# Moving the transposes, the query load and one combination in the attention rows of a hybrid transformer layer

## Chip, cores and metric

The kernel runs on one core of a Trainium2 chip. The metric is device time in microseconds (us) of one execution. Median of three runs before: 2978.12 us (2976.74 to 2979.64).

Engine names are those of the profile: PE is TensorE (matrix products; PEld its weight loads), DVE is VectorE, ACT is ScalarE, POOL is GpSimd, SP is SyncE, which issues most DMA transfers. Each engine executes its own instructions in the order in which the program gives them. PE writes to PSUM, which has eight banks of 512 floats on each of 128 partitions.

## What is computed

One transformer layer, for 256 prompt tokens and 2048 latent tokens. A joint projection gives q, k, v and Fourier channels; the first three go through differential attention, the Fourier channels through a two-dimensional DFT; then come an output projection, a residual, and a squared-ReLU feed-forward net. Latent tokens attend to 512 cached and 2048 latent keys. The part of the reference that the change touches is this:

```python
def one_block(qblk):
    s = jnp.einsum('bqhmd,bkhmd->bhmqk', qblk, k).astype(jnp.float32) * scale
    p = jax.nn.softmax(s, axis=-1)
    a = p[:, :, 0] - lam * p[:, :, 1]
    return jnp.einsum('bhqk,bkhe->bqhe', a.astype(v.dtype), v)
```

There are 4 heads, two score maps m for each head (head dimension 64), and values of width 128. All data are float32; products are made from a high and a low part of one operand or of both (fp32r), so that a float32 product takes several passes.

## The kernel before, in words

The program runs through projection and DFT, attention (from about 568 to 1325 us of the profile), output projection and feed-forward net. The change lies in attention alone.

**Rows and steps.** Attention for the latent tokens has 32 rows: 4 heads by 8 groups of 256 queries (class Group; tile names such as Ss, P0s, pts carry no row number in the profile). A row has two halves j of 128 queries and two maps m, so four softmax sets of 128 x 2560 scores. A set is made in five blocks of 512 keys:

- `fill` (L920): two matmuls on PE into one PSUM bank S. The tag S has five banks, one for each block of a set, so block n of a set can be written when block n of the set before has been read by its exponential.
- `rowmax` (L925): DVE reduces each block to its maximum. `comb` (L928) combines five maxima and negates.
- `exp` (L944): ACT writes exp(S - max) into P0 (m = 0) or P1 (m = 1) and sums it.

After both maps of a half, `combine` forms P0 + factor x P1: small operations on DVE (L948, L949), the factor (L950) and a square (L951), and then the large part. On POOL that is a tensor_scalar (L966) and an addition (L967), first on columns 0 to 1023, then on 1024 to 2559. For the first `vcomb` blocks of 512 columns of the second half of a row, DVE does it instead with one operation a block (L956). `vcomb` is 5 in the very first row and in the very last, 0 elsewhere.

Then the combined weights are transposed and multiplied by the values. `tr` (L976) transposes four 128 x 128 squares on PE into one bank pts (the tag has two banks): one call is a group of two key tiles. `ah` (L982) copies that bank on ACT, `al` (L987) subtracts the copy on DVE to get the low part, and `mul` (L86 to L88, or L1001 and L1008 for two groups that go in one float32 product) multiplies into the bank po.

At a row's end, `o1` (L1012) copies po on ACT, `o2` (L1016) transposes it on PE, `o3` (L1020) copies it on DVE, `o4` (L1026) squares and sums it on ACT (two operations with their sums), `o5` (L1029, L83) and `o6` (L1035) normalise it, and SP stores it to att (L1036). `qload` (L897) has SP load the 256 queries of a row into one of three buffers Q. The prompt's own small attention (class Prompt, one row a head) is woven in between.

**Order.** The order is written out by hand: every call is added to a list with a planned time, and the list, sorted by that time, is the order in which each engine gets its instructions (`manual_schedule`). T is the planned length of a step and u = T / 5. Only the sequence follows from these times; nothing waits for a clock. A row takes four steps. While a row's four sets are made, the sets of the next row are already under way and those of an earlier row are transposed and multiplied; the loop `for q in range(4)` lays a row's ten transpose groups over four steps:

- Step A (q = 0): key tiles 0 and 2; step B (q = 1): 4, 6, 8; step C (q = 2): 10 and 12; step D (q = 3): 14, 16, 18. The number is `kb`, the first of two key tiles.
- In A and C PE makes the five blocks of a later row's set with m = 1 (KS1s) while ACT makes exponentials with m = 0 (P0s); in B and D it is the other way round (KS0s, P1s).
- Products of a step's groups come at the end of the step after it. `o4` of an earlier row comes in step C, behind the second copy `ah`.

PE's order in a step before the change is then: block 1, block 2, first transposes, blocks 3 and 4, second transposes, block 5, (B and D: third transposes), products. In B `o2` follows the first transposes. The planned times that set it, in units of u from the step's start, are blocks at 0.76, 1.42, 2.08, 2.74 and 3.40, and the transposes at:

```python
tr_t, ah_t, al_t = [1.5, 2.8], [3.3, 3.8], [4.6, 5.2]              # A and C
tr_t, ah_t, al_t = [1.5, 2.8, 3.86], [3.3, 3.8, 4.4], [None, 4.6, 5.2]   # B and D
```

Of the kernel before, what the change touches and what calls it, by code (L numbers as in the profile page):

```python
# [40 lines left out]
def body(tc, a, out):  # L41
    nc = tc.nc
    ctx = ExitStack()
    with ctx:
# [796 lines left out]
        with ExitStack() as c3_:  # L841
# [12 lines left out]
            class Head:  # L854
                def __init__(self, s, h):
                    self.s, self.h, self.nm = s, h, f"{'sp'[s]}{h}"
                    self.nk = NK[s]
                    self.nkt, self.nbk = self.nk // P, (self.nk + 511) // 512
                    self.ng = (NS, NP)[s] // 256
                    self.tok0 = (NP, 0)[s] // P  # L860
                    self.hc = slice(h * P, h * P + P)
# [21 lines left out]
            class Group:  # L883
                def __init__(self, hd, g):
                    self.hd, self.g, self.nm = hd, g, f"{hd.nm}_{g}"
                    self.S, self.mx, self.sm, self.p0, self.p1, self.tot = {}, {}, {}, {}, {}, {}
                    self.pt, self.A = {}, {}
                    self.po, self.half = None, []
                    self.nmul = 0
                    self.edge = 20 * g - 1 if hd.h == hd.s == 0 and g < 2 else None  # L890
                    self.last = hd.h == H - 1 and g == NS // 256 - 1

                    self.vcomb = 5 if self.last else 5 if hd.h == hd.s == g == 0 else 0

                def qload(self):
                    self.Q = at.tile([P, 2, 2, 256], F32R, tag="Q", name=f"Q{self.nm}", bufs=3)
# [196 lines left out]
            def add(t, fn, *args):  # L1093
                ev.append((t, len(ev), fn, args))

            T = TSTEP
            u = T / 5.0
# [11 lines left out]
            for h in range(H):  # L1109
                hd, hp = Head(0, h), Head(1, h)  # L1110
                base = h * 32 * T
                add(base - 18 * T + 0.7 if h else -3.04 * T, hd.load_k)
                add(base - 14 * T + 0.7 if h else 0.9 * T, hd.load_v)
                add(base - 13 * T + 0.7 if h else 0.91 * T, hp.load_k)
                add(base - 13 * T + 0.71 if h else 0.92 * T, hp.load_v)
                gp, r = Prompt(hp, 0), base + 10 * T
                add(r - 2 * T, gp.qload)
                for j in range(2):
                    for t, fn in ((5.25, gp.scores), (5.85, gp.rowmax), (6.33, gp.exp), (8.0, gp.combine)):
                        add(r + t * u, fn, j)  # L1120
                    r += 2 * T
                for t, fn, *args in ((5.25, gp.tr, 0), (6.33, gp.ah), (6.95, gp.al), (15.25, gp.mul), (16.33, gp.o1),
                                     (25.25, gp.o2), (25.9, gp.o3), (27.32, gp.o4), (28.557, gp.o5), (29.0, gp.o6)):
                    add(r + t * u, fn, *args)
                for g in range(hd.ng):
                    gr = Group(hd, g)
                    add(base - 2 * T + 0.6 * u if base else -3.03 * T, gr.qload)
                    for st in range(4):
                        j, m = divmod(st, 2)
                        t0 = base + st * T  # L1130
                        for b in range(hd.nbk):
                            add(t0 - T + (0.76 + 0.66 * b) * u, gr.fill, j, m, b)
                            add(t0 - T + (1.26 + 0.66 * b) * u, gr.rowmax, j, m, b)
                            add(t0 + 0.66 * b * u, gr.exp, j, m, b)
                        add(t0 - 0.45 * u, gr.comb, j, m)
                        if m:
                            add(t0 + 5.9 * u, gr.combine, j)
                    kbs = list(range(0, hd.nkt, 2))
                    for q in range(4):
                        w = base + (AVS + q) * T  # L1140
                        if q % 2 == 0:
                            order = [kbs.pop(0) for _ in range(2)]
                            tr_t, ah_t, al_t = [1.5, 2.8], [3.3, 3.8], [4.6, 5.2]
                        else:
                            order = [kbs.pop(0) for _ in range(3)]
                            tr_t, ah_t, al_t = [1.5, 2.8, 3.86], [3.3, 3.8, 4.4], [None, 4.6, 5.2]
                        for n, kb in enumerate(order):
                            add(w + tr_t[n] * u, gr.tr, kb)
                            add(w + ah_t[n] * u, gr.ah, kb)
                            if al_t[n]:  # L1150
                                add(w + al_t[n] * u, gr.al, kb)
                            add(w + T + (3.9 + 0.01 * n) * u, gr.mul, kb)
                            if q == 3 and not n:
                                add(w + 3.95 * u, gr.mul_part, kb)
                    w = base + (AVS + 5) * T + 1.0 * u
                    for t, fn in ((0, gr.o1), (0.75, gr.o2), (0.95 if gr.last else 4.25, gr.o3), (8.5, gr.o4), (9.2, gr.o5), (9.6, gr.o6)):
                        if gr.last and t > 5:
                            LASTO.append(fn)
                        else:
                            add(w + t * u, fn)  # L1160
                    base += 4 * T
# [340 lines left out]
        with c5r, ExitStack() as c5:  # L1502
# [155 lines left out]
            with tc.manual_schedule():  # L1658
                for n, (q, p) in enumerate(ITEMS):
# [10 lines left out]
                    fn, args = FINISH.get(n, (None, ()))  # L1670
# [61 lines left out]
        with ExitStack() as c6:  # L1732
# [62 lines left out]
            with tc.manual_schedule():  # L1795
                pend, NM, loaded, KS = None, 7 * 24, 4, []
                for i in range(7):
                    for b in range(3):
                        ps = [pp.tile([P, 512], F32, tag="ps", name=f"ps{i}_{b}_{j}", bufs=6) for j in range(3)]
                        for k in range(16):  # L1800
# [19 lines left out]
                            if (i, b) == (6, 2) and 9 <= k < 12:  # L1820

                                j = k - 9
                                u = U3[6 + j]
# [14 lines left out]
                for j in range(3):  # L1838
                    t = 6 + j
# [76 lines left out]
```

## Time and profile before

| what | us |
|---|---|
| median of three runs | 2978.12 |
| profiled execution, its own time | 2977.31 |
| its span from first to last instruction | 2975.5 |
| PE busy | 2914.6 |
| DVE busy | 2025.9 |
| ACT busy | 1580.1 |
| POOL busy | 1022.5 |
| attention 800 to 900 us: PE, DVE, ACT, POOL busy of 100 | 97.75, 88.94, 89.51, 89.89 |
| attention 567 to 600 us: PE, DVE, ACT, POOL busy of 33 | 23.77, 27.56, 22.07, 9.71 |

Busy times are shares of the span on which an engine executes something. Matmuls overlap in PE's pipeline and their ends are modelled, so PE's busy time is no measure of how much of its peak it reaches. The chain of work that ended last is followed back from the last instruction, at each point to what released it or to the instruction before it on the same engine; what is not on it has slack. In a timeline, several equal instructions stand in one line (x4 = four of them) with the start of the first and the time until the end of the last, and square brackets give the idle time ahead of them and who ended it. A block of scores is two matmuls, so x2 is one block, x4 two.

### The profile page before, as it was taken

What the parts mean: (1) busy time and instruction counts of PE and PEld (TensorE: products, weight loads), DVE (VectorE), ACT (ScalarE), POOL (GpSimd) and SP (SyncE); (2) the same over time, 40 slices, a digit from 0 to 9 for tenths busy, and PEclk for the clock granted to TensorE, in tenths of its full rate; (3) what the DMA queues carried; (4) which work ended last, traced back from release to release, by engine and by line L of the source; (5) the groups of instructions that cost most, each with busy time, mean ns of one, the idle gap of its engine ahead of it and who ended that gap; (6) DMA issues with size and microseconds to landing.
All of it is one profiled execution on the core that took longest, in us unless ns stands there. A gap on an engine that the chain in (4) does not pass through costs nothing.

```text
span 2975.5 us, 43868 instructions
## 1 busy us (share of the span) xinstructions
PE 2914.6 (98%) x15481; PEld 2512.7 (84%) x15481; DVE 2025.9 (68%) x3379; ACT 1580.1 (53%) x3540; POOL 1022.5 (34%) x839
## 2 busy tenths in 40 slices
PE   8999999999999999999999999999999999999999
PEld 5888887778888888878888999999999888888887
DVE  6666775789888888865458778777776344344554
ACT  4333322688888889964346556556555322232221
POOL 1111112178888988851222333333332000000000
PEclk9999999999999999999999999999999999999999
DMA  7777878512120121215686677676666454445563
GB/s 274 204 195 205 226 195 250 193 52 76 42 110 28 70 84 35 86 58 157 202 251 215 218 239 226 219 238 214 221 200 228 145 171 162 138 145 174 195 215 106
DMA packets 394413, 495.58 MB, mean 167 GB/s; under 512 B 26403, under 2 KB 307056, under 8 KB 391122
## 3 DMA queue, kind: packets, MB, share of 16 engines
q1 hardware_dynamic: 386560, 477.63, 50.4%
q0 software_dynamic: 2992, 7.28, 0.8%
q10 hardware_dynamic: 4642, 7.88, 0.8%
q8 instruction: 122, 2.00, 0.3%
q14 instruction: 97, 0.79, 0.1%
HBM read 315.20 MB, written 179.57 MB: 166 GB/s over the span
## 4 chain that ended last, share of the span: by engine, by line
PE 90%; DVE 3%; ACT 2%; DMA 2%; issue 1%; POOL 1%; SPq 0%; ACTq 0%; DVEq 0%; POOLq 0%
PE Ss L920 10%; PE ps L86 8%; PE ps L87 8%; PE ps L88 8%; PE pj L86 4%; PE pj L88 4%; PE pj L87 4%; PE pts L976 4%; PE po L88 4%; PE po L86 4%; PE po L87 4%; PE pA L1542 2%; PE pA L1543 2%; PE pB L1542 2%; PE pA L1544 2%; PE pC L1544 2%
## 5 line engine op out<-in xcount | busy, mean ns | idle before, releaser
L925 DVE TENSOR_REDUCE mxs<-Ss 128x1 f32<-128x512 f32 x640 | 421.8, 687 | 80.4 <-PE Ss L920 69.9
L1237 DVE TENSOR_TENSOR sl<-sr,sh 128x768 fp32r<-128x768 f32 x168 | 161.7, 963 | 339.9 <-ACT sh L1236 339.4
L967 POOL TENSOR_TENSOR P0s<-P0s,P1s 128x1024 f32<-128x1024 f32 x124 | 365.3, 2946 | 10.3
L1236 ACT CAST sh<-sr 128x768 fp32r<-128x768 f32 x168 | 140.2, 835 | 424.9 <-PE ps L87 424.9
L1584 POOL TENSOR_TENSOR gs<-g,g 128x384 f32<-128x384 f32 x48 | 70.2, 1464 | 483.3 <-ACT g L1554 392.3
L944 ACT ACTIVATE P1s<-Ss,mxs 128x512 f32<-128x512 f32 x320 | 217.3, 694 | 35.6 <-DVE mxs L928 33.4
L86 PE MATMUL pj<-wh,hh 128*128 128x512 f32 x576 | 229.6, 399 | 0.7 <-ACT fo L374 0.7
L87 PE MATMUL ps<-tlT,sh 128*128 128x512 f32 x585 | 229.3, 392 | 0.0
L86 PE MATMUL ps<-thT,sh 128*128 128x512 f32 x585 | 229.2, 392 | 0.0
L87 PE MATMUL pj<-wl,hh 128*128 128x512 f32 x576 | 227.5, 395 | 0.5 <-DVE wl L496 0.5
L88 PE MATMUL ps<-thT,sl 128*128 128x512 f32 x585 | 227.7, 389 | 0.0
L88 PE MATMUL pj<-wh,hl 128*128 128x512 f32 x576 | 226.4, 394 | 0.0
L944 ACT ACTIVATE P0s<-Ss,mxs 128x512 f32<-128x512 f32 x320 | 215.8, 696 | 6.5 <-DVE mxs L928 6.3
L920 PE MATMUL Ss<-KS0s,Qs 128*128 128x512 f32 x640 | 201.8, 424 | 16.9 <-ACT P1s L944 15.6
L920 PE MATMUL Ss<-KS1s,Qs 128*128 128x512 f32 x640 | 210.9, 434 | 4.8 <-ACT P0s L944 4.0
L976 PEld LDWEIGHTS pts<-ident,P0s 128*128 128x128 f32 x1280 | 159.1, 141 | 45.4 <-ACT ahs L982 2.8
L976 PE MATMUL pts<-ident,P0s 128*128 128x128 f32 x1280 | 191.7, 273 | 3.4 <-DVE als L987 1.8
L1553 ACT ACTIVATE g<-uz 128x384 f32<-128x384 f32 x144 | 75.8, 527 | 207.3 <-DVE uz L1576 180.7
L982 ACT CAST ahs<-pts 128x512 fp32r<-128x512 f32 x256 | 151.3, 593 | 47.9 <-PE pts L976 39.7
L987 DVE TENSOR_TENSOR als<-pts,ahs 128x512 fp32r<-128x512 f32 x256 | 165.8, 681 | 11.5 <-ACT ahs L982 11.5
L966 POOL TENSOR_SCALAR P1s<-P1s,tots 128x1024 f32<-128x1024 f32 x124 | 166.8, 1346 | 5.6
L86 PE MATMUL ps<-ophT,sh 128*128 128x512 f32 x423 | 165.9, 392 | 1.1 <-DVE uz L1576 1.1
(615 smaller groups left out, 8248.2 us busy)
## 6 DMA issues: line engine op xcount, KB each, us to landing
sr<-sd SPq DMA_DIRECT2D x84, 768.0 KB, 4.4
a<-in_w SPq DMA_DIRECT2D x184, 256.0 KB, 4.0
sd<-gs SPq DMA_DIRECT2D x192, 192.0 KB, 1.9
sd<-g SPq DMA_DIRECT2D x144, 192.0 KB, 4.0
wm<-in_w_mod SPq DMA_DIRECT2D x32, 512.0 KB, 4.9
Qs<-qd SPq DMA_DIRECT2D x32, 512.0 KB, 3.5
b<-in_w SPq DMA_DIRECT2D x64, 256.0 KB, 4.9
b<-tsum SPq DMA_DIRECT2D x64, 256.0 KB, 4.6
```

The source lines that it names most:

```text
L86: nc.tensor.matmul(ps, lh, rh, start=first, stop=False)
L87: nc.tensor.matmul(ps, lh, rl, start=False, stop=False)
L88: nc.tensor.matmul(ps, ll, rh, start=False, stop=last)
L920: nc.tensor.matmul(S[:, :w], self.Q[:, x, m, j * P:j * P + P], self.hd.KS[m][:, b * 512:b * 512 + w], start=(x == 0), stop=(x == 1))
L925: nc.vector.tensor_reduce(self.mx[j][:, m, b:b + 1], self.S[j, m, b], axis=AX.X, op=ALU.max)
L944: nc.scalar.activation(dst, S, AF.Exp, bias=self.mx[j][:, m, 6:7], accum_out=self.sm[j][:, m, b:b + 1])
L966: nc.gpsimd.tensor_scalar(p, p, tot[:, 3:4], 0.0, op0=ALU.mult, op1=ALU.add)
L967: nc.gpsimd.tensor_add(d, d, p)
L976: nc.tensor.transpose(pt[:, c:c + P], self.p0[j][:, (kb + t) * P:(kb + t + 1) * P], ident)
L982: nc.scalar.copy(t, self.pt[kb])
L987: nc.vector.tensor_sub(t, self.pt[kb], f32(self.A[kb][0]))
L1237: nc.vector.tensor_sub(lo, src, f32(hi))
```

## The change

- The first transposes of every step are planned at 2.1 u instead of 1.5 u, which is behind the third score block instead of the second. In A and C the second transposes are planned at 3.45 u instead of 2.8 u, behind the fifth block instead of the fourth.
- `o2` is planned 0.4 u later (1.15 instead of 0.75), so it stays behind the first transposes of step B; in the last row `o3` moves along (1.35 instead of 0.95).
- `qload` is planned one step earlier (base - 3 T instead of base - 2 T) in all rows but the first.
- In the very first row `vcomb` is 2 instead of 5: DVE combines columns 0 to 1023 of the second half with two operations, POOL columns 1024 to 2559 with L966 and L967.

In the built program PE's order differs by these exchanges in 31 steps A and 30 steps each of B, C and D, DVE has three operations fewer (L956) and POOL two more, ACT's order is the same, and on SP's queue a query load now stands ahead of the two stores of att that came before it.

```diff
-                    self.vcomb = 5 if self.last else 5 if hd.h == hd.s == g == 0 else 0
+                    self.vcomb = 5 if self.last else 2 if hd.h == hd.s == g == 0 else 0
...
-                    add(base - 2 * T + 0.6 * u if base else -3.03 * T, gr.qload)
+                    add(base - 3 * T + 0.6 * u if base else -3.03 * T, gr.qload)
...
-                            tr_t, ah_t, al_t = [1.5, 2.8], [3.3, 3.8], [4.6, 5.2]
+                            tr_t, ah_t, al_t = [2.1, 3.45], [3.3, 3.8], [4.6, 5.2]
...
-                            tr_t, ah_t, al_t = [1.5, 2.8, 3.86], [3.3, 3.8, 4.4], [None, 4.6, 5.2]
+                            tr_t, ah_t, al_t = [2.1, 2.8, 3.86], [3.3, 3.8, 4.4], [None, 4.6, 5.2]
...
-                    for t, fn in ((0, gr.o1), (0.75, gr.o2), (0.95 if gr.last else 4.25, gr.o3), (8.5, gr.o4), (9.2, gr.o5), (9.6, gr.o6)):
+                    for t, fn in ((0, gr.o1), (1.15, gr.o2), (1.35 if gr.last else 4.25, gr.o3), (8.5, gr.o4), (9.2, gr.o5), (9.6, gr.o6)):
```

## The prediction

> **What bounds the kernel now.** I read the page first: engine totals, then the chain of work that ended last. TensorE (PE) is busy 98% of the span and is 90% of that chain, so only what shortens or lengthens PE's own order of work counts.
>
> ```profile
> PE   2914.6 (98%) x15481; PEld 2512.7 (84%) x15481; DVE 2025.9 (68%) x3379; ACT 1580.1 (53%) x3540; POOL 1022.5 (34%) x839
> ...
> PE 90%; DVE 3%; ACT 2%; DMA 2%; issue 1%; POOL 1%; SPq 0%; ACTq 0%; DVEq 0%; POOLq 0%
> ```
>
> All edits lie in attention, so I next took the same chain in order of time over a few rows (a row is 256 queries of one head). Columns: start, length, what. A row has four steps; A and C transpose two groups (pts), B and D three. Shown are the first two score blocks of A, B, C, D and of the next A (775.79 is C), with all of C up to its fifth block.
>
> ```profile
> 764.78 1.12 PE Ss L920 x4
> ...
> 770.20 1.21 PE Ss L920 x4
> ...
> 775.79 1.40 PE Ss L920 x4
> 777.19 0.44 PE pts L976 x4
> 777.62 0.93 PE Ss L920 x4
> 778.55 0.44 PE pts L976 x4
> 778.99 0.46 PE Ss L920 x2
> ...
> 781.73 0.97 PE Ss L920 x4
> ...
> 787.00 1.18 PE Ss L920 x4
> ```
>
> Two score blocks (x4, two matmuls each) cost 0.93 when nothing holds them, 0.465 a block; a transpose group costs 0.435. The opening pairs of A, B, C, D take 1.12, 1.21, 1.40 and 0.97, so they hold waits of 0.19, 0.28, 0.47 and 0.04: 0.98 us a row. A row takes 787.00 - 764.78 = 22.22, so 21.24 is PE work and 0.98 is all that better order could win: at most 30 us over 30 to 31 rows.
>
> What the pair waits for is seen in the timeline of a step C and the start of its D (start, length, engine, line; brackets give idle time and who ended it).
>
> ```profile
> 800.40 2.05 DVE L925 TENSOR_REDUCE mxs<-Ss 128x1 f32<-128x512 f32 x3 [0.21 <-PE Ss L920]
> ...
> 800.67 0.60 PE L976 MATMUL pts<-ident,P0s 128*128 128x128 f32 x4
> ...
> 801.02 0.71 PE L920 MATMUL Ss<-KS1s,Qs 128*128 128x512 f32 x2
> ...
> 801.36 0.59 ACT L982 CAST ahs<-pts 128x512 fp32r<-128x512 f32 x1 [0.20 <-PE pts L976]
> ...
> 802.27 0.31 ACT L1026 ACTIVATE osqs<-os 128x128 f32<-128x128 f32 x1
> ...
> 802.49 0.19 ACT L1026 ACTIVATION_READ_ACCUMULATOR osqs<-os 128x1 f32 x1
> 802.49 0.16 DVE L928 TENSOR_REDUCE mxs<-mxs 128x1 f32<-128x5 f32 x1
> ...
> 802.74 0.69 ACT L944 ACTIVATE P1s<-Ss,mxs 128x512 f32<-128x512 f32 x1
> ...
> 803.42 0.68 ACT L944 ACTIVATE P1s<-Ss,mxs 128x512 f32<-128x512 f32 x1
> ...
> 804.24 0.30 PEld L920 LDWEIGHTS Ss<-KS0s,Qs 128*128 128x128 f32 x2 [0.21 <-ACT P1s L944]
> ```
>
> There are five score banks, so block n of a step needs block n of the step before to have been exponentiated: the second exp ends at 804.10, the second block's weights start at 804.24. Exps follow each other every 0.67 to 0.68 (802.74, 803.42). The first exp waits for the combined maximum (802.49), that for the last of five reduces, and that for the fifth block: three reduces from 800.40 in 2.05 put the last start near 801.76, 0.74 after the fifth block's 801.02. So the loop is: fifth block, reduce, maximum, exps, next step's second block. Its other side is PE's work from the fifth block to that second block.
>
> **First transposes behind the third block.** Instruction counts on PE stay; the built order swaps places in 31 steps A and 30 each of B, C and D (while the last rows are transposed there are no scores left), and ScalarE's order is unchanged. Before, the first transposes (0.435) stood between the second and third block, so the third came 0.465 + 0.435 = 0.90 after the second, later than the exps' 0.67. Now it can come 0.465 after, and its bank is free 0.67 after: where the second block waited, the third waits another 0.205, and the transposes that could fill it stand behind it. The fourth follows at 0.90, past its exp. The earlier third reduce wins nothing if the last reduce hangs on the fifth block. Cost: +0.205 in A, +0.205 in C. The second output transposes (o2) move along in B, at no change of work.
>
> **Second transposes behind the fifth block (A and C).** The fifth block comes earlier relative to PE's remaining work by 0.435. The reduces now limit by a little: five with their data there take 3.09, 0.60 apart, while the blocks are 0.465 apart, so 0.135 is lost.
>
> ```profile
> 804.88 3.09 DVE L925 TENSOR_REDUCE mxs<-Ss 128x1 f32<-128x512 f32 x5
> ```
>
> So the second block of the following step (B, D) waits 0.30 less. In B: 0.28 goes to nothing with 0.02 to spare, and its third block then waits 0.205 - 0.02 = 0.185; gain 0.095. In D 0.04 would go, but ScalarE interferes. The second copy (ahs) cannot start before the second transposes, and they start later: in C the third block moves from 0.90 to 0.67 behind the second, then come transposes 0.435, two blocks 0.93, so they start 0.67 + 0.465 + 0.435 + 0.93 = 2.50 behind the second block, before 0.90 + 0.93 = 1.83: 0.67 later. In A the queue has room.
>
> ```profile
> 813.72 0.69 ACT L944 ACTIVATE P1s<-Ss,mxs 128x512 f32<-128x512 f32 x1 [0.86 <-DVE mxs L928]
> ```
>
> There 0.86 of idle time stands ahead of the first exp, so 0.67 fits. In C the two squares (L1026) are queued on ScalarE between that copy and the first exp; the queue is free at 802.49 + 0.19 = 802.68 and the exp starts at 802.74, so 0.06 is the whole room. The exp goes 0.67 - 0.06 = 0.61 later, PE's own work of C only 0.205 later: the wait in D grows by 0.61 - 0.205 = 0.405, and its third block adds 0.205: +0.61. What waits behind that exp is all of D's exps and through them D's blocks.
>
> Sum for a row: 0.205 - 0.095 + 0.205 + 0.61 = +0.925. In four of the 30 full rows the prompt's exps lie in D and PE waits there already; I take two thirds, 0.6. 26 x 0.925 + 4 x 0.6, and 0.205 for the odd A, make **+26.7 us**. Bounds: without the squares' delay D loses its 0.04, (0.205 - 0.095 + 0.205 - 0.04) a row +0.275, in all 30 x 0.275 + 0.205 = +8.5; with the prompt's rows whole, 30 x 0.925 + 0.205 = +28.0.
>
> **The shared combination.** Only the first row. Timeline of the start, then the windows (length, busy times, granted clock, DMA share, GB/s):
>
> ```profile
> 572.68 2.08 PE L920 MATMUL Ss<-KS1s,Qs 128*128 128x512 f32 x6 [1.37 <-ACT P0s L944]
> ...
> 583.24 0.16 DVE L928 TENSOR_REDUCE mxs<-mxs 128x1 f32<-128x5 f32 x1
> ...
> 584.35 1.55 POOL L966 TENSOR_SCALAR P1s<-P1s,tots 128x1536 f32<-128x1536 f32 x1
> ...
> 585.99 3.48 POOL L967 TENSOR_TENSOR P0s<-P0s,P1s 128x1536 f32<-128x1536 f32 x1
> ...
> 587.09 0.16 DVE L928 TENSOR_REDUCE mxs<-mxs 128x1 f32<-128x5 f32 x1
> ...
> 587.86 4.82 DVE L956 SCALAR_TENSOR_TENSOR P0s<-P1s,tots,P0s 128x512 f32<-128x512 f32 x5
> ...
> 595.71 0.16 DVE L928 TENSOR_REDUCE mxs<-mxs 128x1 f32<-128x5 f32 x1
> ...
> 596.81 1.22 PE L920 MATMUL Ss<-KS0s,Qs 128*128 128x512 f32 x2 [5.29 <-ACT P1s L944]
> ```
>
> ```profile
> 567.00:587.00 20.00, 17.29 (x60) 8.84 (x58) 16.98 (x32) 15.15 (x42) 6.65 (x6) 1.00 0.75 274
> ...
> 597.00:601.00 4.00, 3.11 (x6) 1.43 (x6) 1.51 (x4) 2.44 (x8) 0.00 (x0) 0.50 0.00 0
> ```
>
> ```profile
> 601.65 0.16 DVE L928 TENSOR_REDUCE mxs<-mxs 128x1 f32<-128x5 f32 x1
> ...
> 608.58 0.16 DVE L928 TENSOR_REDUCE mxs<-mxs 128x1 f32<-128x5 f32 x1
> ...
> 614.10 0.16 DVE L928 TENSOR_REDUCE mxs<-mxs 128x1 f32<-128x5 f32 x1
> ```
>
> VectorE's five block operations hold the reduces for 4.82. Three of them go: 3 x 0.964 = 2.89, and PE's idle gap falls from 5.29 to 2.40. After the gap of 5.29 the granted clock is 0.50 and steps are slow: the maxima come at 595.71, 601.65 and 608.58, where earlier steps without transposes took 587.09 - 583.24 = 3.85 and the next one with transposes 614.10 - 608.58 = 5.52. At full clock they would come at 592.82, 596.67 and 602.19: 6.4 us sooner. The bounds are 2.89 (clock still halved) and 6.4. A gap of 2.40 is nearer to 1.37, which stood in a stretch at clock 1.00, than to 5.29, so I take **-6.4**.
>
> The Trainium skill's page "TensorE: Matmul & The Clock Gate", Part 1, has the clock halved once a whole window of about 3.4 us was idle; the 0.50 behind the 5.29 gap agrees, and no run here yet shows a gap of 2.40. By that rule the term is -6.4; if the clock halves all the same, -2.89 and the total is 3000.2.
>
> GpSimd (POOL) takes the last 1536 columns: 1.55 + 3.48 = 5.03, behind the addition that ends at 585.99 + 3.48 = 589.47 and a small square: about 590.2 to 595.3. It sat idle there, and its next combination (602.18) moves only to about 597.2. The first transposes (604.55) move to about 599. So it is covered; a loss would need over 1.9 us more.
>
> ```profile
> 602.18 0.34 POOL L950 TENSOR_SCALAR tots<-tots,nlam 128x1 f32<-128x1 f32 x1 [12.03 <-DVE tots L949]
> ```
>
> ```profile
> 604.55 1.05 PE L976 MATMUL pts<-ident,P0s 128*128 128x128 f32 x4
> ```
>
> **Queries sooner.** One load a row on SP's queue goes ahead of the two stores of att, which wait there for GpSimd; nothing waits for those stores in attention. In the list of waits PE waited for queries three times:
>
> ```profile
> PE Ss L920 <- DMA Qs<-qd: 0.9, 3, 0.4
> ```
>
> At most **-0.9**, taken whole; the buffer a load asks for was last read in a step before the request, so I see no loss.
>
> **Sum.** The profiled execution took 2977.31 (span 2975.5 and 1.8 around it), 0.8 below the median 2978.12. 2977.31 + 26.7 - 6.4 - 0.9 = **2996.7**.
>
> **Rivals.**
> 1. The exps of D are not held up (the squares or the copy leave more room than 0.06). A row costs +0.275: 2977.31 + 8.5 - 7.3 = 2978.5. For it: only C shows the tight queue. Against: 802.68 to 802.74.
> 2. Faster: VectorE sets the pace. Every step shows about 0.21 idle before its third reduce (800.40); if the maximum follows the third block, not the fifth, 0.21 comes off every step's loop, and the third block's own wait goes with it. The waits 0.19, 0.28, 0.47, 0.04 fall by up to 0.21 each, 0.19 + 0.21 + 0.21 + 0.04 = 0.65 a row, 30 rows 19.5: 2977.31 - 19.5 - 7.3 = 2950.5. It decides as soon as the last reduce no longer starts 0.74 behind the fifth block. Against: that 0.74.
> 3. The steady cost stands, but the start wins only 2.89: 3000.2.
> That the change does not take place is no case: the built order has the swaps.
>
> **How the numbers follow.** Forecast 0.50 (own range 2990 to 3006), rival 1 0.20 (2973 to 2985), rival 2 0.13 (2945 to 2965), rival 3 0.12, anything beyond 3006 0.05. From 2972 to 3006 lies 0.50 + 0.20 + 0.12 = 0.82. About 0.2%, 6 us, is what a measurement of this kernel can tell from no change, so same is 2972.2 to 2984.1. Slower: 0.50 + 0.12 + 0.05 and a little of rival 1, 0.68; same 0.17; faster rival 2 with its neighbours, 0.15.
>
> **What would show it.** Right: in the chain, the opening three blocks (x6, 1.395 without waits) are longer by 0.40 in A, 0.68 in C and 0.65 in D; the first exp behind C's squares starts at once behind them; a row takes 23.1 to 23.2; the start has no 0.50 clock. Wrong: a row at or below 22.2, or the first exp behind C still released by the maximum, or the clock still halved at 595.

## The result, and the profile after

| | before | after |
|---|---|---|
| median, us | 2977.89 (2976.66 to 2979.64, 6 runs) | 2998.15 (2996.97 to 2999.91, 6 runs) |
| span of the profiled execution, us | 2975.5 | 2996.0 |

The kernel is slower by 20.3 us: ratio 1.0068, 95% interval 1.0055 to 1.0081. The chain of work that ended last has changed its make-up: before, PE had 90% of it, DVE 3% and ACT 2%; now ACT and DVE have 4% each. Page of the kernel after, engine totals and chain:

```profile
PE 2938.4 (98%) x15481; PEld 2508.9 (84%) x15481; DVE 2028.9 (68%) x3376; ACT 1582.6 (53%) x3540; POOL 1027.3 (34%) x841
...
PE 89%; DVE 4%; ACT 4%; DMA 2%; issue 1%; POOL 0%; SPq 0%; ACTq 0%; DVEq 0%; POOLq 0%
```

PE's busy time went up by 23.8 us for the same 15481 matmuls, since most of a block's wait for its bank stands in the profile as busy time: in the opening of step D shown below (784.37 to 786.32), which holds 0.555 of waiting, PE counts as busy throughout. The chain of after in order of time, from a step A to the next A (start, length, what); now three blocks (x6) open a step. An exponential is two instructions, the activation and the read-out of its sum, so x4 on ScalarE is two of them:

```profile
766.87 1.78 PE Ss L920 x6
...
769.60 1.30 DVE mxs L925 x2
...
771.17 1.45 ACT P1s L944 x4
772.62 0.32 ACT oTs L1012
772.94 0.69 ACT P1s L944 x2
...
773.67 0.73 PE Ss L920 x2
...
774.83 0.22 PE po L1016 x2
...
778.26 2.06 PE Ss L920 x6
...
784.37 1.95 PE Ss L920 x6
...
790.20 1.78 PE Ss L920 x6
```

Without waits three blocks take 1.395. So the opening waits are 1.78 - 1.395 = 0.385 in A, 0.665 in C (778.26) and 0.555 in D (784.37); before they were 0.19, 0.47 and 0.04. In B the chain runs through ScalarE: two exps, the output copy (L1012), the third exp, and only then the third block at 773.67. The row takes 790.20 - 766.87 = 23.33 instead of 22.22.

To see where the 20.5 us between the spans lie, I took the distances between the 128 combined maxima (L928 in the timeline) of each kernel. "Prompt rows" are the three rows a head beside which the prompt's attention runs; "full rows" are the other 17 that come after the first.

| stretch | before | after | difference |
|---|---|---|---|
| up to the first maximum | 571.66 | 572.07 | +0.4 |
| start, to the seventh maximum | 29.99 | 28.02 | -2.0 |
| first row with transposes | 23.43 | 23.26 | -0.2 |
| 12 prompt rows | 283.8 | 288.7 | +5.0 |
| 17 full rows | 380.0 | 397.3 | +17.3 |
| the rest | 1686.7 | 1686.6 | -0.1 |

Of the 17.3, A gives -1.7, B +7.3, C -1.7 and D +13.5. (These lie between maxima, so work that moved behind a step's fifth block, such as the second transposes (0.435) of A and C, counts in the next step.)

The row in more detail: a step B and the end of a C in the timeline of after. Columns: start, length, engine, line, what; brackets give idle time and its releaser.

```profile
772.37 1.09 PE L920 MATMUL Ss<-KS0s,Qs 128*128 128x512 f32 x4
...
772.56 0.37 ACT L1012 COPY oTs<-po 128x256 f32<-128x256 f32 x1
772.83 0.69 ACT L944 ACTIVATE P1s<-Ss,mxs 128x512 f32<-128x512 f32 x1
...
773.67 0.73 PE L920 MATMUL Ss<-KS0s,Qs 128*128 128x512 f32 x2 [0.22 <-ACT P1s L944]
...
782.22 0.58 ACT L982 CAST ahs<-pts 128x512 fp32r<-128x512 f32 x1 [0.78 <-PE pts L976]
...
782.59 0.16 DVE L928 TENSOR_REDUCE mxs<-mxs 128x1 f32<-128x5 f32 x1
...
783.36 0.19 ACT L1026 ACTIVATION_READ_ACCUMULATOR osqs<-os 128x1 f32 x1
...
783.45 0.67 ACT L944 ACTIVATE P1s<-Ss,mxs 128x512 f32<-128x512 f32 x1
```

In C ScalarE sits idle 0.78 before the copy ahs, waiting for its transposes, the maximum is there at 782.75, but ScalarE is still in the squares, whose last part starts at 783.36, and the first exp follows that at once, at 783.45. The groups of the page say it for all rows: ScalarE's idle time ahead of these copies doubled. First before, then after:

```profile
L982 ACT CAST ahs<-pts 128x512 fp32r<-128x512 f32 x256 | 151.3, 593 | 47.9 <-PE pts L976 39.7
```

```profile
L982 ACT CAST ahs<-pts 128x512 fp32r<-128x512 f32 x256 | 149.7, 587 | 94.4 <-PE pts L976 93.9
```

The start of after, timeline, then windows (length, busy of PE, PEld, DVE, ACT, POOL, granted clock, DMA share, GB/s):

```profile
586.39 3.51 POOL L967 TENSOR_TENSOR P0s<-P0s,P1s 128x1536 f32<-128x1536 f32 x1
...
588.26 2.85 DVE L956 SCALAR_TENSOR_TENSOR P0s<-P1s,tots,P0s 128x512 f32<-128x512 f32 x2
...
594.13 0.16 DVE L928 TENSOR_REDUCE mxs<-mxs 128x1 f32<-128x5 f32 x1
...
595.24 1.22 PE L920 MATMUL Ss<-KS0s,Qs 128*128 128x512 f32 x2 [3.31 <-ACT P1s L944]
```

```profile
592.00:597.00 5.00, 1.22 (x2) 0.50 (x2) 3.95 (x8) 2.59 (x8) 3.95 (x2) 0.71 0.00 0
597.00:601.00 4.00, 2.08 (x4) 1.12 (x4) 1.96 (x6) 1.58 (x7) 0.34 (x1) 0.50 0.00 0
```

The gap of 5.29 became 3.31, and the granted clock still went to 0.50, as in before.

### The profile page after: what moved, and what is told of

Read it like the earlier page. It is cut to its first block, busy times and chain, and to the rows that moved or that the text cites. A ratio compares the mean times of both kernels' runs of the same rounds, so it can differ in the third digit from the quotient of the medians.

```text
span 2996.0 us, 43807 instructions
## 1 busy us (share of the span) xinstructions
PE 2938.4 (98%) x15481; PEld 2508.9 (84%) x15481; DVE 2028.9 (68%) x3376; ACT 1582.6 (53%) x3540; POOL 1027.3 (34%) x841
## 4 chain that ended last, share of the span: by engine, by line
PE 89%; DVE 4%; ACT 4%; DMA 2%; issue 1%; POOL 0%; SPq 0%; ACTq 0%; DVEq 0%; POOLq 0%
PE Ss L920 10%; PE ps L86 8%; PE ps L87 8%; PE ps L88 8%; PE pj L88 4%; PE pj L87 4%; PE pj L86 4%; PE pts L976 4%; PE po L86 4%; PE po L88 4%; PE po L87 4%; ACT P1s L944 2%; PE pA L1542 2%; PE pB L1542 2%; PE pB L1543 2%; PE pB L1544 2%
## 5 line engine op out<-in xcount | busy, mean ns | idle before, releaser
L967 POOL TENSOR_TENSOR P0s<-P0s,P1s 128x1536 f32<-128x1536 f32 (+1 forms) x125 | 369.0, 2952 | 10.4
L920 PE MATMUL Ss<-KS0s,Qs 128*128 128x512 f32 x640 | 211.3, 431 | 14.4 <-ACT P1s L944 14.4
L966 POOL TENSOR_SCALAR P1s<-P1s,tots 128x1536 f32<-128x1536 f32 (+1 forms) x125 | 168.2, 1346 | 5.7
```

What stands on the lines that cost most here:

```text
L920: nc.tensor.matmul(S[:, :w], self.Q[:, x, m, j * P:j * P + P], self.hd.KS[m][:, b * 512:b * 512 + w], start=(x == 0), stop=(x == 1))
L966: nc.gpsimd.tensor_scalar(p, p, tot[:, 3:4], 0.0, op0=ALU.mult, op1=ALU.add)
L967: nc.gpsimd.tensor_add(d, d, p)
```

## The experiments

The theory is that of the forecast: the loop from fifth block through reduce, maximum and exps to the next step's blocks sets the pace, the third block now waits for its exponential, and ScalarE's queue holds the exps of D. The main rival is that VectorE's reduces set the pace, so that an earlier third block helps. A theory on the start (its gap and the half clock) stands beside them. A, B, C and D are lengths of a step between combined maxima in the full rows, unless an opening or a wait is named. Every comparison is with the kernel before unless "against after" is said; beside the experiments the kernel before took 2977.87 (first four), 2978.51 (next four), 2978.38 (step A alone and both added up) and 2979.55 (the last).

### One part alone

**Combination alone** (before, with this line):

```diff
-                    self.vcomb = 5 if self.last else 5 if hd.h == hd.s == g == 0 else 0
+                    self.vcomb = 5 if self.last else 2 if hd.h == hd.s == g == 0 else 0
```

> Before with the shared combination alone. The prediction's own step said 6.4 us faster, by way of a PE gap of 2.40 and a clock that stays full. The trace of the changed kernel speaks for another size: its two block operations took 2.85 together (the two that lie beside GpSimd's addition), so the three that went were the short ones, 1.97; its PE gap was 3.31 and the clock still fell to 0.50. By that: 2.0 to 2.4 faster, about 2975.7.

Measured: 2976.51, ratio 0.9996 (0.9987 to 1.0004). The gap is 3.30, and the sixth maximum comes 22.05 after the first instead of 24.05, so 2.0 is won there. The granted clock in the windows from 597 on is 0.66, 0.50 and 0.64, longer below full than in after, and the first row's steps are slow for it: A 7.75 instead of 6.93. The expected 2.0 to 2.4 came at the start, but the total can't be told from no change.

**Queries alone** (before, with this line):

```diff
-                    add(base - 2 * T + 0.6 * u if base else -3.03 * T, gr.qload)
+                    add(base - 3 * T + 0.6 * u if base else -3.03 * T, gr.qload)
```

> Before with the earlier query load alone. By the list of waits, 0.9 us faster. Rival: more waits are hidden in it, put down to ScalarE. In a step B of the trace of before (PE at 748.02) the first score block starts 0.7 after the exp it names, and 4.56 after its query load was issued (743.46); rows of that kind take 22.6 instead of 22.25. If these are late queries, some 12 rows gain 0.35 each: 4 to 6 us faster, about 2973.

Measured: 2978.23, ratio 1.0002 (0.9993 to 1.0011). The 17 full rows take 378.5 instead of 380.0: in before, five of them have a B of 5.86 to 6.24 instead of 5.77, here one. Between these two traces late queries cost 1.5, more than the list of waits had shown, because a late row was put down to ACT there. The amount is not fixed: with the loads where before has them, the 17 rows took 379.1 with the combination alone, and 380.3 in the run further down that gives the combination to GpSimd. The total shows no gain, neither 0.9 nor the 4 to 6 of the rival; the first row had a longer stretch of half clock (25.31 instead of 23.43).

**First transposes alone** (before, with o2 and o3 moved along):

```diff
-                            tr_t, ah_t, al_t = [1.5, 2.8], [3.3, 3.8], [4.6, 5.2]
+                            tr_t, ah_t, al_t = [2.1, 2.8], [3.3, 3.8], [4.6, 5.2]
...
-                            tr_t, ah_t, al_t = [1.5, 2.8, 3.86], [3.3, 3.8, 4.4], [None, 4.6, 5.2]
+                            tr_t, ah_t, al_t = [2.1, 2.8, 3.86], [3.3, 3.8, 4.4], [None, 4.6, 5.2]
```

> Before with the first transposes behind the third block in all four steps (and the output transposes with them), second ones left. Theory (score blocks paced by the exps through five banks): the third block waits 0.205 more in A, B, C and D, and in B another 0.33, since the output copy (L1012, 0.37) stands on ScalarE between the second and the third exp: 0.8 to 1.15 a row, 25 to 35 us slower, 3003 to 3012. Rival (VectorE's reduces set the pace, the third reduce comes sooner): 10 to 20 us faster.

Measured: 3000.44, ratio 1.0075 (1.0063 to 1.0088). Chain of this kernel, the openings of C, D and A:

```profile
784.70 2.06 PE Ss L920 x6
...
790.84 1.64 PE Ss L920 x6
...
796.32 1.84 PE Ss L920 x6
```

Less 1.395 they wait 0.665, 0.245 and 0.445, and before 0.47, 0.04 and 0.19: 0.20 to 0.26 more, which is the exp's 0.67 less the block's 0.465. The steps between maxima grew by 0.20 in A, C and D and by 0.44 in B. VectorE's third reduce now follows the second without the 0.21 of idle time (that stands ahead of the fourth and fifth instead), and the time goes up, so the rival that VectorE sets the pace falls. This edit alone costs as much as the whole change.

**Second transposes alone** (before, with this line):

```diff
-                            tr_t, ah_t, al_t = [1.5, 2.8], [3.3, 3.8], [4.6, 5.2]
+                            tr_t, ah_t, al_t = [1.5, 3.45], [3.3, 3.8], [4.6, 5.2]
```

> Before with the second transposes behind the fifth block in A and C alone. Theory: B gains 0.2 (its second block no longer waits, its third waits a little on the output copy), D loses 0.40, since the copy behind the second transposes and the two squares behind that copy hold ScalarE's next exps 0.46 later with 0.06 of room: 0.2 a row slower, 4 to 8 us, about 2984. Rival without the squares: D loses nothing, a row gains 0.24, 7 us faster, 2971.

Measured: 2985.9, ratio 1.0022 (1.0013 to 1.0032). A and C get shorter (means 5.47 to 5.29 and 5.52 to 5.34), D goes from 5.51 to 6.15: the hold on D's exps is there without the first transposes. The four parts alone are -1.4, +0.4, +22.6 and +8.0, together about 30, and the change is 20.3. In D both the third block's wait and the held exps fall on the same time (0.20 and 0.64 alone, 0.78 together), and A and C, longer in the one run and shorter in the other, come out 0.1 shorter.

### One hold taken away from after

**Squares ahead of C's second copy** (after, with `o4` moved):

```diff
-                    for t, fn in ((0, gr.o1), (1.15, gr.o2), (1.35 if gr.last else 4.25, gr.o3), (8.5, gr.o4), (9.2, gr.o5), (9.6, gr.o6)):
+                    for t, fn in ((0, gr.o1), (1.15, gr.o2), (1.35 if gr.last else 4.25, gr.o3), (7.5, gr.o4), (9.2, gr.o5), (9.6, gr.o6)):
```

> The changed kernel with the two squares (o4) moved ahead of the second copy of step C, into ScalarE's 0.78 of idle time there. Theory: D's exps are held by the copy and the squares behind it; now only 0.9 - 0.78 = 0.1 is left, so D's interval between combined maxima falls from 6.30 to about 5.8 and a row wins 0.4 to 0.5: 12 to 15 us under the changed kernel, about 2984. Rival (D is long because of the score blocks alone): no change, 2998.

Measured: 2986.64, ratio 1.0028 (1.0016 to 1.0039), 11.5 less than after. The opening of D in this kernel's chain:

```profile
786.31 1.39 PE Ss L920 x6
```

D's wait is gone (1.39 is three blocks without any), and D falls from 6.30 to 5.74; A, B and C keep their lengths. So the squares behind a later copy are what holds D.

**Output copy behind the third exp in B** (after, with `o1` and `o2` moved; the last row as it was):

```diff
-                    for t, fn in ((0, gr.o1), (1.15, gr.o2), (1.35 if gr.last else 4.25, gr.o3), (8.5, gr.o4), (9.2, gr.o5), (9.6, gr.o6)):
+                    for t, fn in ((0 if gr.last else 1.7, gr.o1), (1.15 if gr.last else 2.88, gr.o2), (1.35 if gr.last else 4.25, gr.o3), (8.5, gr.o4), (9.2, gr.o5), (9.6, gr.o6)):
```

> The changed kernel with the output copy (o1, L1012) moved from between the second and third exp of step B to behind the fifth, and o2 behind the third transposes. Theory: B's third block waits on the third exp, which that copy holds up by 0.33; B's interval falls from 6.27 to about 5.97: 8 to 10 us under the changed kernel, about 2989. Rival (B's excess comes from the block order alone): no change, 2998.

Measured: 2991.65, ratio 1.0040 (1.0028 to 1.0053), 6.5 less than after. The opening of B, now in one piece, in the chain and then in PE's timeline:

```profile
776.19 1.54 PE Ss L920 x6
```

```profile
776.03 1.70 PE L920 MATMUL Ss<-KS0s,Qs 128*128 128x512 f32 x6
```

B's wait by the chain is 1.54 - 1.395 = 0.145. In the timeline the three blocks take 1.70, where after had them from 772.37 to 773.67 + 0.73 = 774.40, in 2.03: the copy of 0.37 between the second and third exp cost 0.33. B falls from 6.27 to 5.72, by 0.55; the other 0.22 is what o2 takes on PE, which now stands behind the fifth block and fills a part of C's wait there (C opens with 1.84 instead of 2.06). The total gained less than these rows, because in this trace the first row took 25.89 instead of 23.26, with the clock below full for longer.

### The start

**The whole first combination on GpSimd** (before, with this line):

```diff
-                    self.vcomb = 5 if self.last else 5 if hd.h == hd.s == g == 0 else 0
+                    self.vcomb = 5 if self.last else 0
```

> Before with the first row's combination wholly on GpSimd (vcomb 0). It tests the start: without the 4.82 on VectorE the PE gap of 5.29 should shrink to about 0.5 and the granted clock stay at 1.00; maxima of the first steps 3.85 apart; the combined weights come only near 599, which the first transposes may wait for. Theory (gap and half clock cost the start 4.8 + 3): 4 to 8 us faster, 2970 to 2974. Rival (the late combination is waited for): no gain or a loss of some us.

Measured: 2975.19 (2969.91 to 2978.1), ratio 0.9983 (0.9974 to 0.9991). PE's timeline and the windows of this kernel:

```profile
592.18 0.72 PE L920 MATMUL Ss<-KS0s,Qs 128*128 128x512 f32 x2 [0.54 <-ACT P1s L944]
594.18 1.41 PE L920 MATMUL Ss<-KS0s,Qs 128*128 128x512 f32 x4 [1.29 <-ACT P1s L944]
597.38 2.07 PE L920 MATMUL Ss<-KS1s,Qs 128*128 128x512 f32 x4 [1.79 <-ACT P0s L944]
```

```profile
592.00:597.00 5.00, 2.13 (x6) 0.90 (x6) 2.88 (x7) 3.25 (x11) 4.92 (x3) 0.99 0.00 0
597.00:601.00 4.00, 3.62 (x12) 2.96 (x13) 1.51 (x3) 3.59 (x11) 3.74 (x5) 0.59 0.00 0
601.00:605.00 4.00, 2.13 (x11) 1.25 (x10) 3.38 (x7) 2.36 (x6) 3.92 (x3) 1.00 0.39 131
```

The longest gap ahead of it is 1.79, and the clock still falls to 0.59 for a while. The seventh maximum comes 24.56 after the first instead of 29.99, 5.4 sooner; GpSimd keeps up. The median gains 3.3, a little less than expected; this trace is of the fastest execution.

### A better order

**Order reworked** (before, with four edits: queries as in the change; A and C with the second transposes behind the fifth block and the first where they were; squares ahead of the copy; output copy later):

```diff
-                    add(base - 2 * T + 0.6 * u if base else -3.03 * T, gr.qload)
+                    add(base - 3 * T + 0.6 * u if base else -3.03 * T, gr.qload)
...
-                            tr_t, ah_t, al_t = [1.5, 2.8], [3.3, 3.8], [4.6, 5.2]
+                            tr_t, ah_t, al_t = [1.5, 3.45], [3.3, 3.8], [4.6, 5.2]
...
-                    for t, fn in ((0, gr.o1), (0.75, gr.o2), (0.95 if gr.last else 4.25, gr.o3), (8.5, gr.o4), (9.2, gr.o5), (9.6, gr.o6)):
+                    for t, fn in ((0 if gr.last else 1.7, gr.o1), (0.75 if gr.last else 2.88, gr.o2), (0.95 if gr.last else 4.25, gr.o3), (7.5, gr.o4), (9.2, gr.o5), (9.6, gr.o6)):
```

> Before with the earlier query load, second transposes behind the fifth block in A and C, squares ahead of C's second copy, output copy behind the fifth exp of B; first transposes stay behind the second block. Theory: second transposes win about 0.1 to 0.2 a row in B once the squares and the output copy hold up nothing; late queries go: 5 to 10 us faster than before, 2968 to 2973. Rival (second transposes cost as such, as alone, +7): 2985.

Measured: 2975.53, ratio 0.9991 (0.9982 to 0.9999), less of a gain than expected. A full row takes 22.03 instead of 22.27, but D is 5.80 instead of 5.52, and the 12 prompt rows lose 2.2. The openings of C and D in its chain, and C's third to fifth block, show what D's length is:

```profile
775.82 1.22 PE Ss L920 x4
...
777.48 1.56 PE Ss L920 x6
...
781.72 0.92 PE Ss L920 x4
```

D opens without any wait (0.92 for two blocks), so nothing holds it: it is longer between maxima because C's second transposes now count in it. What this order costs stands in C, and likewise in A: the third to fifth block take 1.56 instead of 1.395. They follow each other without transposes between them, 0.465 apart where the exps are 0.67 apart; the fifth waits for the exp that frees its bank, and about 0.17 of waiting comes back there.

**Step A alone** (before, with the output copy as above, the combination on GpSimd, queries 3 steps ahead, squares where they were):

```diff
-                            tr_t, ah_t, al_t = [1.5, 2.8], [3.3, 3.8], [4.6, 5.2]
+                            tr_t, ah_t, al_t = [1.5, 2.8 if q else 3.45], [3.3, 3.8], [4.6, 5.2]
```

> The kernel before with four edits: the first row's whole combination on GpSimd; queries a step sooner; the second transposes behind the fifth block in step A alone (C as before, so the squares keep their place); the output copy and its transposes in B later, behind the third exponential. Theory that each step pays for its own holds (the third block behind the exponentials, ScalarE's queue ahead of the next ones): A 5.30 and B 5.6 as in the run with the order reworked, C 5.51 and D 5.52 as in the kernel before, because nothing of D's hold is made; a full row 21.95 instead of 22.26 and no row with a late query. Against the run with the order reworked (30 rows 684.3) D gives back 0.28 and C takes 0.17 more in 30 rows: about 681, 6 below the kernel before; with the start of the run that gave the combination to GpSimd, about 3 more: near 2969. Rival: the gains of the separate runs do not add, since the start's stretch of half clock and the prompt's rows take them back: 2973 to 2976, with the rows above 684.

Measured: 2970.22, ratio 0.9971 (0.9960 to 0.9981). The time is near the expected 2969. A 5.29, C 5.51 and D 5.52 came as expected, but six full rows had a B of 5.97 to 6.83 instead of 5.6, and the 30 rows took 686.5 instead of 681. In such a row the timeline names the queries:

```profile
745.10 1.19 PE L920 MATMUL Ss<-KS0s,Qs 128*128 128x512 f32 x4 [0.94 <-DMA Qs<-qd]
```

**Both added up** (the order reworked, with this line):

```diff
-                    self.vcomb = 5 if self.last else 5 if hd.h == hd.s == g == 0 else 0
+                    self.vcomb = 5 if self.last else 0
```

> The run with the order reworked (queries a step sooner, second transposes of A and C behind the fifth block, the squares ahead of C's second copy, the output copy and its transposes later) with the first row's whole combination on GpSimd added. If start and rows are separate, the gains of the two runs add: 2.9 and 3.3 below the kernel before, near 2972, rows 684 in all, D 5.80. Rival, that the start's earlier maxima are lost again in the first full row's half clock: 2975, like either of the two alone.

Measured: 2971.29, ratio 0.9976 (0.9967 to 0.9986). It is 7.1 below the kernel before, where the two gains alone add up to 6.3: start and rows look separate, though each of these differences is uncertain by some 3. The rows took 685.8, 1.5 above the run with the order reworked, in the first row and in a few late steps B.

**Queries 3.2 steps ahead** (step A alone, with this number):

```diff
-                    add(base - 3 * T + 0.6 * u if base else -3.03 * T, gr.qload)
+                    add(base - 3.2 * T + 0.6 * u if base else -3.03 * T, gr.qload)
```

> The run with step A alone, with one number changed: the queries are asked for 3.2 steps ahead instead of 3. At 3 steps a load and the stores of att have the same planned time, and which stands first on SP's queue is decided by rounding: in 11 of 28 rows the load goes ahead of the two stores, in 17 it stays behind them as before. At 3.2 it goes ahead in all 28. In the run with step A alone, rows 8, 10, 14, 15, 22 and 24 have a step B of 5.97 to 6.83 instead of 5.6, and all six are rows whose load stayed behind. Theory that these are late queries: all full rows take 5.6 in B, the 30 rows 681.5 instead of 686.5, and the time is 5 less, near 2965. Rival, that these steps wait for something else (a bank of scores or the output copy, which now comes behind the third exponential): some of them stay, and the time is 2970 as before.

Measured: 2967.37 (2965.2 to 2969.63), ratio 0.9961 (0.9948 to 0.9975): the fastest kernel of the study, some 12 us below the kernel before. The 30 rows took 681.2, and no B in a full row is over 5.79. Against the kernel before it gains 12.2 where step A alone gained 8.2, so 4.0 more where 5 was expected. That difference is about as large as its uncertainty; the profile decides: the six late steps, 4.8 over 5.6 in all, are gone. Openings of D, A, B and C in its chain, with A's third to fifth block:

```profile
751.67 0.97 PE Ss L920 x4
...
756.94 1.16 PE Ss L920 x4
...
758.53 1.58 PE Ss L920 x6
...
762.62 0.93 PE Ss L920 x4
...
767.85 1.20 PE Ss L920 x4
```

Two blocks without waits take 0.93, so the opening waits are 0.04, 0.23, 0 and 0.27, against 0.04, 0.19, 0.28 and 0.47 before; in A another 1.58 - 1.395 = 0.185 stands in the third to fifth block.

## Why the forecast was right, and which of its steps failed

The time came out 1.5 us above the forecast of 2996.7, and by its mechanism: the third block waits, and the squares hold D. But that it came so close is in part luck: the terms for B, for the rows with the prompt and for the start were mis-sized, and they nearly cancel. A full row takes 23.33 where 23.1 to 23.2 was forecast.

1. **First transposes, +0.205 a step: right.** The opening waits in A and C are 0.385 and 0.665, the forecast had 0.40 and 0.68; the first transposes alone show about 0.2 in A, C and D.
2. **D, +0.61: the mechanism is right,** its wait of 0.555 was put at 0.65. The exp behind the squares starts at once, as the forecast asked; moving the squares ahead of the copy gives back 11.5. D grew by 0.515, 0.095 less than the 0.61, and the step that missed is the room of 0.06 on ScalarE. It was reckoned from the end of the squares' read-out, but an exp starts 0.09 after the start of the read-out in front of it (783.36 and 783.45 in after). By that the queue was free at 802.49 + 0.09 = 802.58, the room was 0.16, and the term comes to 0.51.
3. **B, -0.095: wrong.** The forecast had the wait of B go from 0.28 to 0.185, as if each exp followed the one before by 0.67. In B the output copy stands between the second and third exp, and as soon as the third block waits for the third exp, the copy is in the loop. B's wait is then 0.145 + 0.33 = 0.475 with its two parts from the run that moved the copy, so it grew by 0.195 where a gain of 0.095 was forecast. The forecast had costed `o2` on PE and never looked at what `o1` does on ScalarE.
4. **Rows with the prompt: mis-sized.** Only four rows were taken at less, but 12 are disturbed; they lose 0.41 each, the full rows 1.02. In before their B was already 6.25 to 6.68 (a full row's is 5.77), and D in two of three was 6.19 to 7.25; that the new waits fall on these is likely, but was not tested. All 30 rows lost 22.1 (with about 1.5 won by the queries inside it), against 26.7.
5. **Shared combination, -6.4: wrong, -2.0 measured.** The first failing step is "3 x 0.964". The average of five operations hid that one of them was unlike the others. The view of the line L956 (minimum, median, maximum in ns), before:

```profile
L956 DVE SCALAR_TENSOR_TENSOR P0s<-P1s,tots,P0s x10: 737/746/2167, 587.9 to 1306.0; 128x512 f32<-128x512 f32 x10
```

   One took 2.17, and two operations in after take 2.85, so the three that went were worth 4.82 - 2.85 = 1.97. The long one stayed; GpSimd's addition runs beside the first of the two (586.39 to 589.90 in after, the pair from 588.26). The gap is then 5.29 - 1.97 = 3.32, not 2.40, and the rival "the start wins only 2.89" is what happened, with a lower bound that was itself too high. The second failing step is the one from a shorter gap to a full clock, worth 3.5 of the 6.4. The forecast's own sign of being wrong came: in after the clock is 0.50 from 595 on. A gap of 2.40 was not tried, but with the combination on GpSimd the clock fell with no gap longer than 1.79 ahead of it, so 2.40 was no ground for a full clock. The Trainium skill's page "GPSIMD Engine Reference", Specifications, says that GpSimd shares its SBUF interfaces with VectorE and contends with instructions of VectorE that have two SBUF inputs; the 2.17 against 0.75 agrees with it. No run here took the addition away from beside that one operation, but in the very last row, where no GpSimd addition runs beside them, all five took about 0.75 (five in 3.40).
6. **Queries, -0.9: about right, for another reason.** The row of the waits list was only a part; about 1.5 in the trace of before was hidden in steps put down to ScalarE, and other traces with the same loads have more or less of it. And the statement that a load goes ahead of the two stores holds for 11 of 28 loads only: at 3 steps load and stores have the same planned time, and rounding, or where the sums are equal to the last digit the place in the list, leaves 17 loads behind. At 3.2 steps all 28 go ahead.
7. **Rival 1** (D not held) and **rival 2** (VectorE paces) fall: D is held in the second transposes alone and freed by the squares' move, and an earlier third reduce won nothing. **Rival 3** (a small gain at the start) is what the start did, with 2.0 in place of 2.89.

Open: why exactly the prompt rows lose less, and how much late queries cost a kernel on the average of its executions.

## What to carry to other kernels

In a loop over a few banks, filler work on PE earns most where the next block would otherwise wait: moved behind that block, as the first transposes here, it hides nothing any more, and three blocks in a row without filler can outrun the exps again (0.17 in the reworked order). Before an operation is moved on one engine, look at what stands between the releasing instructions on the other engine (here a copy between two exps, and squares behind a copy), since a new wait brings those into the loop. Take a part's duration from minimum, median and maximum rather than from the mean, and don't let two entries of a hand-written order have the same planned time.

## What was not expected of the hardware

- **The clock fell after shorter gaps than expected.** A PE gap of 3.31 was followed by a granted clock of 0.50, and gaps of 0.54, 1.29 and 1.79, with PE busy for 2.13 of 5 us, by 0.59. By windows of one us the fall lies inside a gap: in after the clock is 1.00 from 593 to 594 and 0.57 from 594 to 595, which puts the fall some 2.2 into the gap of 3.31; with the combination on GpSimd it is 0.95 from 596 to 597 and 0.50 from there, some 1.3 into the gap of 1.79. These two positions are estimates from the windows' means. The Trainium skill's page "TensorE: Matmul & The Clock Gate" has the clock halve after an idle window of about 3.4 us (Part 1), and its section "Why this matters for your kernels" advises against gaps above about 3. The 3.31 lies between the two, and the 1.79 under both, so the trace does not agree with a rule that goes by single gaps. No run here tells single gaps from the busy share of a stretch.
- **The half clock lasts differently from run to run.** The same page says that the window runs freely, so that its effect varies; the trace agrees. The first row's steps A, with the same work in them, took 6.93 in before, 7.75 with the combination alone and 7.32 with the queries alone. The whole first row took 23.43, 25.85 and 25.31, so an experiment on the start has to be read against some 2 us of this.
- **A VectorE operation beside a GpSimd addition took 2.17 us** instead of 0.75. A tiny one shows it more clearly. The operation of L1029 (`o5`, 128 x 2, both inputs in SBUF) takes 0.15 to 0.16 in before with no GpSimd operation beside it, and up to 1.25 otherwise: in 34 of its 36 executions one of L966 or L967 was already running, and each time it ended within 0.03 of that one's end. So in that trace such an operation is not finished before GpSimd's is. It costs no time here: in before, full rows with 1.21 and with 0.29 for it both take 22.26.
